# Own buffers for two tiles and one order edge in the seven-product pairs of a decoder layer

## The chip, the cores and the metric

The kernel runs on one core of a Trainium2 chip. A core has five engines that run beside one another, each with its own list of instructions that it takes in order: TensorE (PE, matrix products), VectorE (DVE), ScalarE (ACT), GpSimd (POOL) and SyncE (SP, which here issues loads and nothing else). Transfers between the memory of the chip and the core's own memory (SBUF) are done by 16 DMA engines; SyncE's and GpSimd's queues feed them. TensorE writes into PSUM, eight banks of 512 float32 in each of 128 partitions. The metric is the device time of one execution in microseconds (us); lower is better.

## The reference

One decoder layer on 512 tokens of width 1024 in float32: an input projection, block-sparse causal attention with a learned bias beside a causal mean-pool mixer, a gated merge and an output projection, a layer norm, and then the part that matters here, a gated MLP with 2816 inner channels and a causal convolution of width 3 on the gate:

```python
a, u = jnp.split(h @ w_ffn_in[l], 2, axis=-1)      # each (512, 2816)
a = causal_dwconv(a, conv_w[l], conv_b[l])
f = (jax.nn.gelu(a, approximate=False) * u) @ w_ffn_out[l]
h = layer_norm(ALPHA * h + f, ln2_g[l], ln2_b[l])
```

## The kernel before

Every product is made in three passes to keep float32 accuracy on faster matmuls: an operand is split into a high half (a rounded copy, by ScalarE) and a low half (what the copy lost, by VectorE), and TensorE adds high x high, high x low and low x high. So each weight tile of 128 x 1024 goes through the same path: a load into a raw buffer (tag `wraw`, three slots), a copy into `whi` by ScalarE (line 69), a difference into `wlo` by VectorE (line 70), and then matmuls. `whi` and `wlo` are rings of five slots each. The helper `split` issues the two, `mm3` (lines 182 to 186) the three matmuls.

The 2816 channels of `a` and of `u` are 22 tiles of 128. Tile f of `a` and tile f of `u` make a pair. Pairs 0 to 3 and 18 to 21 are computed plainly. For the pairs 4 to 17 (`SEVEN`) the two products are seen as one product of 2 x 2 blocks, the weights of `a` and `u` cut by the upper and lower half of the 1024 inputs and the tokens by halves of 256, and it is made with seven block products in place of eight, as Winograd and Strassen do. `seven(f)` (line 693) issues them, each of 12 matmuls of 256 columns. A pair needs four weight tiles:

- A: the weights of `a`, loaded (line 146).
- X: a sum of both weights, made by the DMA in two legs: a load of the weights of `u` by SyncE (line 131), and an accumulating load of the weights of `a` by GpSimd (line 132). It has a pool of its own, tag `xraw`, two slots. `fetch_sums` issues it some tiles ahead.
- D: the "quarter", half a tile of the weights of `u`, loaded (line 146), 128 x 512.
- Y: A plus parts of X, made by two sums of VectorE (line 144). The first needs X and A, the second A.

A, D and Y share the three slots of `wraw`. In the text the tile A of pair 12 is called A12, and so on. In the order of the loop a pair uses A, X, Y, A again, D, X again; the second use of Y, the closing product, is kept in the list `pending` and issued in the next pair. A and X have two products, Y two, D one.

The products land in three banks per pair (`sa`, `sb`, `sc`). The first product is copied by ScalarE into half of `y`, one of two tiles that alternate between pairs and that later hold the gate's convolution and activation (`gated`, lines 623 to 628). VectorE adds the parts (lines 708 to 711, "small adds"), the convolution takes two steps (lines 624 and 625) and the product with `u` one (line 628). VectorE also makes some sums of finished tiles for the product behind (lines 757 and 763).

The order of each engine's list isn't the order of the code. The kernel is built by a scheduler that knows what each instruction needs and which slot it takes, estimates times by a model of its own, and places the instructions of all engines by them. A slot is given to the next tile in the scheduler's order, and the wait for its last user is set with a semaphore. `keep_in_program_order` adds an edge: the instruction stays behind the one that was issued before it in the code on the same engine.

Of the kernel before, what the change touches and what calls it, by code (L numbers as in the profile page):

```python
# [8 lines left out]
F32 = mybir.dt.float32  # L9
F32R = mybir.dt.float32r  # L10
AF = mybir.ActivationFunctionType
ALU = mybir.AluOpType
PSUM = bass.MemoryType.PSUM

P = 128
S = 512
D = 1024
# [28 lines left out]
def layer_kernel(ctx: ExitStack, tc: tile.TileContext, xT, x, w_v, w_c, rel_bias, invcnt, w_group,  # L46
                 pscale, w_br, w_out, lnr, w_fi, convp, w_fo, out):
    nc = tc.nc
    const = ctx.enter_context(tc.tile_pool(name="const", bufs=1))
    wp = ctx.enter_context(tc.tile_pool(name="wp", bufs=1))  # L50
# [7 lines left out]
    def bank(name):  # L58
        return ps.tile([P, S], F32, tag="ps", name=name)
# [5 lines left out]
    def split(hi, lo, src, copy=None):  # L65
        if copy:
            copy(hi, src)
        else:
            nc.scalar.activation(hi, src, AF.Copy)  # L69
        nc.vector.tensor_tensor(lo, src, hi.bitcast(F32), op=ALU.subtract)  # L70
# [27 lines left out]
    def fetch(pool=None, early=None):  # L98
        i = state["next"]
        state["next"] = i + 1  # L100
        while sums and xu and fi_at[sums[0], "X"] <= i + AHEAD:
            fetch_sums(sums.pop(0))
        if isinstance(chunks[i], tuple):
            ready[i] = (fetch_fo if i >= FO0 else fetch_seven)(i, *chunks[i])
            return
        raw = wp.tile([P, D], F32, tag="wraw", name=f"wraw{i}", bufs=3)
        if pool is None:
            hi = wp.tile([P, D], F32R, tag="whi", name=f"whi{i}", bufs=RING)
            lo = wp.tile([P, D], F32R, tag="wlo", name=f"wlo{i}", bufs=RING)
        else:  # L110
            hi = pool.tile([P, D], F32R, name=f"whi{i}")
            lo = pool.tile([P, D], F32R, name=f"wlo{i}")
        parts = 2 if early else 1
        for c in range(parts):
            sl = slice(c * (D // parts), (c + 1) * (D // parts))
            (nc.scalar if early else nc.sync).dma_start(raw[:, sl], chunks[i][:, sl])
            split(hi[:, sl], lo[:, sl], raw[:, sl], fast if early and c == 0 else None)
            if c == 0 and early:
                early()
        ready[i] = (hi, lo)  # L120

    raws = {}
    sums = list(SEVEN)
    xu = None

# [9 lines left out]
    def fetch_seven(i, f, q):  # L135
        n = S if q == "D" else D
        if q == "X":
            raw = raws[f, "X"]
        else:
            raw = raws[f, q] = wp.tile([P, D], F32, tag="wraw", name=f"wraw{i}", bufs=3)[:, :n]  # L140
        if q == "Y":
            a, x_ = raws[f, "A"], raws[f, "X"]
            for c, o in ((slice(0, S), x_[:, S:]), (slice(S, D), raw[:, :S])):
                nc.vector.tensor_tensor(raw[:, c], o, a[:, c], op=ALU.add)
        elif q != "X":
            nc.sync.dma_start(raw, w_fi[2 * f] if q == "A" else w_fi[2 * f + 1][:, S:])
        hi = wp.tile([P, D], F32R, tag="whi", name=f"whi{i}", bufs=RING)[:, :n]
        lo = wp.tile([P, D], F32R, tag="wlo", name=f"wlo{i}", bufs=RING)[:, :n]
        split(hi, lo, raw)
        return hi, lo  # L150
# [26 lines left out]
    def weights(i):  # L177
        while state["next"] <= min(i + LEAD, state["limit"]):
            fetch()
        return ready[i]  # L180

    def mm3(out_, w, a, start, stop, **kw):
        (wh, wl), (ah, al) = w, a
        nc.tensor.matmul(out_, wh, ah, start=start, stop=False, **kw)  # L184
        nc.tensor.matmul(out_, wh, al, start=False, stop=False, **kw)  # L185
        nc.tensor.matmul(out_, wl, ah, start=False, stop=stop, **kw)  # L186

    def split3(v, a):
        return tuple(t.rearrange("p (a c) -> p a c", a=a) for t in v)
# [83 lines left out]
    for kt in range(KT):  # L273
        wh, wl = split3(weights(kt // 2), 2)
        wh, wl = wh[:, kt % 2, :], wl[:, kt % 2, :]
        xs_ = [(xT_hi[:, kt, j * P:(j + 1) * P], xT_lo[:, kt, j * P:(j + 1) * P]) for j in range(NT)]
        last = kt == KT - 1
        if last:
            for j in range(NT):
                mm3(bs[j], xs_[j], (wh, wl), False, True)  # L280
                nc.scalar.activation(vv[:, j, :], bs[j], AF.Copy)
        else:
            for n, (a, b) in enumerate(((0, 0), (1, 0), (0, 1))):
                for j in range(NT):
                    nc.tensor.matmul(bs[j], xs_[j][a], (wh, wl)[b], start=kt == 0 and n == 0, stop=False)  # L285
# [50 lines left out]
    def pool_out(j):  # L336
        b = bank(f"zb{j}")
        mm3(b, (wg_hi[:, j, :], wg_lo[:, j, :]), dif[j], True, True)
        nc.scalar.activation(zT[:, j, :], b, AF.Copy, scale=psc[:, j:j + 1])

    def in_tile(n):
        kind, j = order[n]
        wh, wl = split3(weights(C0 + n), KT)
        b = bank(f"{kind}{j}")
        for kt in range(KT):
            mm3(b, (wh[:, kt, :], wl[:, kt, :]), (xT_hi[:, kt, :], xT_lo[:, kt, :]), kt == 0, kt == KT - 1)
        if kind == "q":
            q_done(j, b)
        elif kind == "k":
            k_done(j, b)  # L350
        elif kind == "p":
            pool_in(j, b)
        elif len(gslot) < NKEEP:
            gslot[j] = gates[:, len(gslot), :]
            nc.vector.tensor_copy(gslot[j], b)
        else:
            gslot[j] = late[:, len(gslot) - NKEEP, :]
            nc.scalar.activation(gslot[j], b, AF.Sigmoid)
# [106 lines left out]
    for f in range(KT):  # L465
        if f == KT - LEAD:
            state["limit"] = WO0 + RING - 1
        wh, wl = split3(weights(BR0 + f), KT)
# [31 lines left out]
    ytiles = [ypool.tile([P, S], F32, name=f"y{j}") for j in range(2)]  # L500
# [120 lines left out]
    def gated(j, a, u, sign=None):  # L621
        y = ytiles[j % 2]
        nc.scalar.activation(y, a, AF.Identity, bias=cvp[:, j, 3:4], scale=cvp[:, j, 2:3])
        nc.vector.scalar_tensor_tensor(y[:, 1:], a[:, :S - 1], cvp[:, j, 1:2], y[:, 1:], op0=ALU.mult, op1=ALU.add)  # L624
        nc.vector.scalar_tensor_tensor(y[:, 2:], a[:, :S - 2], cvp[:, j, 0:1], y[:, 2:], op0=ALU.mult, op1=ALU.add)
        nc.scalar.activation(y, y, AF.Gelu)
        if sign:
            nc.vector.scalar_tensor_tensor(fT[:, j, :], y, sign, u, op0=ALU.mult, op1=ALU.mult)
        else:
            nc.vector.tensor_tensor(fT[:, j, :], y, u, op=ALU.mult)  # L630
# [20 lines left out]
    t1, t2 = slice(0, 256), slice(256, 512)  # L651
# [27 lines left out]
    for n in ("nT1", "T3", "nT2", "T4"):  # L679
        t_form(n)  # L680
    state["limit"] = len(chunks) - 1
    pending = []

    def s_mm(f, q, part, act_, b, start, skip=True):
        wh, wl = split3(weights(fi_at[f, q]), 4 if q == "D" else KT)
        for k in range(4):
            mm3(b, (wh[:, 4 * part + k, :], wl[:, 4 * part + k, :]), (act_[0][:, k, :], act_[1][:, k, :]),
                start and k == 0, k == 3, skip_group_check=not start)

    def whole(k, t):  # L690
        return hT_hi[:, k, t], hT_lo[:, k, t]

    def seven(f):
        ba, bb, bc = (bank(f"s{q}{f}") for q in "abc")
        chain, low, c11 = ba[:, 256:], bb[:, :256], bc[:, :256]
        y = ytiles[f % 2]
        u = xu.tile([P, S], F32, tag="u", name=f"u{f}", bufs=2)
        s_mm(f, "A", 0, whole(k1, t1), chain, True)
        nc.scalar.activation(y[:, t1], chain, AF.Copy)
        s_mm(f, "X", 0, tt["T3"], low, True)  # L700
        nc.scalar.activation(u[:, t2], low, AF.Copy)
        if pending:
            pending.pop()()
        s_mm(f, "Y", 0, tt["nT2"], chain, False)
        nc.scalar.activation(u[:, t1], chain, AF.Copy)
        s_mm(f, "A", 1, whole(k2, t1), c11, True)
        s_mm(f, "D", 0, tt["T4"], low, False)
        nc.vector.tensor_tensor(u[:, t1], u[:, t1], low, op=ALU.add)
        s_mm(f, "X", 1, tt["nT1"], chain, False)
        nc.vector.tensor_tensor(u[:, t2], u[:, t2], chain, op=ALU.add)  # L710
        nc.vector.tensor_tensor(ba[:, t1], y[:, t1], c11, op=ALU.add)

        def close():
            s_mm(f, "Y", 1, whole(k2, t2), chain, False)
            gated(f, ba, u, -1.0)

        pending.append(close)
# [3 lines left out]
    xu = xus.enter_context(tc.tile_pool(name="xu", bufs=1, reuse_waits="tile"))  # L721
# [211 lines left out]
```

## Time and profile before

| | |
|---|---|
| median of 3 runs | 650.57 us (650.09 to 651.02) |
| profiled execution | 649.74 us, of which the span from the first to the last instruction is 648.0 |
| TensorE busy | 635.7 us, 98% of the span |
| VectorE, ScalarE, GpSimd busy | 449.5, 328.0, 111.6 us |
| loaded and stored | 94.79 MB |

The profile was taken in one execution by the hardware. A row of the page or of a timeline has the engine, the line of the kernel, the operation and the tiles written and read, with buffer numbers left out (`whi` for each of its tiles); in a timeline the first two numbers are the start and the duration, in us from the start of the span, and brackets hold the idle time of the engine before it and what ended it. The chain of waits follows the work that ended last back to what released each step. A table of windows gives for a stretch the busy time of PE, PE's weight loads, DVE, ACT and POOL, each with its number of instructions in brackets, then the granted clock, the share of the DMA and GB/s. Matmuls are pipelined, so the time from one start to the next says more than their duration.

### The profile page before, as it was taken

The numbers are of one execution on the slowest core, as the hardware profiler recorded it, in microseconds if no ns is written. First come the engines' busy times: TensorE is split into PE (matmuls) and PEld (weight loads), VectorE is DVE, ScalarE is ACT, GpSimd is POOL, SyncE is SP. The second block draws the span as 40 slices with busy tenths as digits, with TensorE's granted clock in tenths as the row PEclk, the third lists the DMA queues.
The fourth block names the chain that finished last, engine by engine and source line by source line (L and its number), as shares of the span: only waits on it lengthen the run. The fifth ranks groups of instructions, "written<-read, shape, count | busy, mean of one in ns | idle before, by whom it ended". The sixth has DMA issues, their size and how long they took to land.

```text
span 648.0 us, 9322 instructions
## 1 busy us (share of the span) xinstructions
PE 635.7 (98%) x3586; PEld 551.4 (85%) x3586; DVE 449.5 (69%) x666; ACT 328.0 (51%) x475; POOL 111.6 (17%) x153
## 2 busy tenths in 40 slices
PE   9999999999999999999999999999999999999994
PEld 6888787877888888888999999998998888888884
DVE  6466665564532576299667888787986859698596
ACT  6547556675522333215444556455665337465452
POOL 1605361211000123300010101010100201123302
PEclk9999999999999999999999999999999999999998
DMA  9643222212222227404056686677635895989905
GB/s 323 197 166 99 82 81 82 74 67 89 74 95 98 91 98 286 136 1 162 2 150 173 170 208 155 179 179 188 165 128 163 274 264 137 218 188 193 282 4 129
DMA packets 32540, 94.79 MB, mean 146 GB/s; under 512 B 3688, under 2 KB 3944, under 8 KB 32240
## 3 DMA queue, kind: packets, MB, share of 16 engines
q1 hardware_dynamic: 22832, 66.91, 30.4%
q0 software_dynamic: 9088, 26.24, 20.7%
q10 hardware_dynamic: 576, 1.05, 0.5%
q8 instruction: 28, 0.46, 0.3%
q14 instruction: 16, 0.13, 0.1%
HBM read 91.02 MB, written 3.17 MB: 145 GB/s over the span
## 4 chain that ended last, share of the span: by engine, by line
PE 91%; DVE 3%; POOL 2%; DMA 1%; ACT 1%; issue 1%; DVEq 0%; ACTq 0%; POOLq 0%
PE fi L186 5%; PE fi L184 5%; PE fi L185 5%; PE g L184 5%; PE g L186 4%; PE g L185 4%; PE sa L184 4%; PE sa L186 4%; PE sa L185 4%; PE v L285 3%; PE wo L186 2%; PE br L186 2%; PE br L184 2%; PE wo L184 2%; PE wo L185 2%; PE br L185 2%
## 5 line engine op out<-in xcount | busy, mean ns | idle before, releaser
L70 DVE TENSOR_TENSOR wlo<-wraw,whi 128x1024 fp32r<-128x1024 f32 (+1 forms) x119 | 144.1, 1214 | 59.2 <-ACT whi L69 57.7
L69 ACT ACTIVATE whi<-wraw 128x1024 fp32r<-128x1024 f32 (+1 forms) x118 | 117.2, 996 | 131.9 <-PE g L185 23.6
L186 PE MATMUL fi<-hT_hi,wlo 128*128 128x512 f32 (+1 forms) x168 | 56.7, 339 | 0.0
L185 PE MATMUL fi<-hT_lo,whi 128*128 128x512 f32 (+1 forms) x168 | 56.7, 339 | 0.0
L184 PE MATMUL fi<-hT_hi,whi 128*128 128x512 f32 (+1 forms) x168 | 56.4, 340 | 0.0
L184 PE MATMUL g<-xT_hi,whi 128*128 128x512 f32 x128 | 50.3, 393 | 0.0
L186 PE MATMUL g<-xT_hi,wlo 128*128 128x512 f32 x128 | 49.9, 390 | 0.0
L185 PE MATMUL g<-xT_lo,whi 128*128 128x512 f32 x128 | 49.8, 389 | 0.0
L132 POOL DMA_DIRECT2D xraw<-in_w_fi x14 | 17.0, 1215 | 183.7 <-DVE y L624 70.2
L69 ACT ACTIVATE whi<-tw 128x1024 fp32r<-128x1024 f32 (+1 forms) x30 | 29.4, 982 | 21.6 <-DMA tw<-in_w_fo 8.1
L70 DVE TENSOR_TENSOR wlo<-tw,whi 128x1024 fp32r<-128x1024 f32 (+1 forms) x30 | 33.3, 1127 | 8.4 <-ACT whi L69 8.4
L185 PEld LDWEIGHTS fi<-hT_lo,whi 128*128 128x128 f32 x168 | 31.9, 190 | 3.5
L186 PEld LDWEIGHTS fi<-hT_hi,wlo 128*128 128x128 f32 x168 | 31.9, 190 | 3.3
L184 PEld LDWEIGHTS fi<-hT_hi,whi 128*128 128x128 f32 x168 | 31.6, 190 | 3.3
L184 PE MATMUL sa<-hT_hi,whi 128*128 128x256 f32 x112 | 31.9, 285 | 2.0 <-ACT whi L69 1.9
L186 PE MATMUL sa<-hT_hi,wlo 128*128 128x256 f32 x112 | 31.7, 284 | 0.0
L185 PE MATMUL sa<-hT_lo,whi 128*128 128x256 f32 x112 | 31.6, 283 | 0.0
L184 PE MATMUL sb<-T_hi,whi 128*128 128x256 f32 x112 | 31.5, 282 | 0.0
L184 PE MATMUL sa<-nT_hi,whi 128*128 128x256 f32 x112 | 31.5, 281 | 0.0
L186 PE MATMUL sa<-nT_hi,wlo 128*128 128x256 f32 x112 | 31.3, 279 | 0.0
L185 PE MATMUL sa<-nT_lo,whi 128*128 128x256 f32 x112 | 31.3, 279 | 0.0
L185 PE MATMUL sb<-T_lo,whi 128*128 128x256 f32 x112 | 31.3, 279 | 0.0
(250 smaller groups left out, 1762.8 us busy)
## 6 DMA issues: line engine op xcount, KB each, us to landing
wraw<-in_w_fi SPq DMA_DIRECT2D x30, 512.0 KB, 3.6
wraw<-in_w_c SPq DMA_DIRECT2D x28, 512.0 KB, 3.4
tw<-in_w_fo POOLq DMA_DIRECT2D x20, 512.0 KB, 8.3
xraw<-in_w_fi SPq DMA_DIRECT2D x14, 512.0 KB, 4.9
xraw<-in_w_fi POOLq DMA_DIRECT2D x14, 512.0 KB, 5.7
wraw<-in_w_fo SPq DMA_DIRECT2D x10, 512.0 KB, 5.1
tw<-in_w_fo SPq DMA_DIRECT2D x10, 512.0 KB, 6.6
wraw<-in_w_br SPq DMA_DIRECT2D x8, 512.0 KB, 3.3
```

The costliest lines, as they stand in the source:

```text
L69: nc.scalar.activation(hi, src, AF.Copy)
L70: nc.vector.tensor_tensor(lo, src, hi.bitcast(F32), op=ALU.subtract)
L132: nc.gpsimd.dma_start(v, bass.AP(tensor=a.tensor, offset=a.offset, ap=[[pst, pn], [u.offset + S - a.offset, 2], [est, S]]), accum_op=ALU.add)
L184: nc.tensor.matmul(out_, wh, ah, start=start, stop=False, **kw)
L185: nc.tensor.matmul(out_, wh, al, start=False, stop=False, **kw)
L186: nc.tensor.matmul(out_, wl, ah, start=False, stop=stop, **kw)
L285: nc.tensor.matmul(bs[j], xs_[j][a], (wh, wl)[b], start=kt == 0 and n == 0, stop=False)
```

## The change

The D tile gets a buffer of its own (`draw`, one slot, in the pool of X), so that `wraw`'s three slots serve A and Y alone. The copy of the first product goes to a tile of its own (`p1`, two slots) instead of half of `y`. The first matmul of D's product gets an order edge on TensorE: it stays behind the matmul before it in the code, the last of the first tile's second product. The list `pending` is made earlier in the code, with no effect. The new buffers take 4 KB of each partition.

```diff
@@ fetch_seven
         if q == "X":
             raw = raws[f, "X"]
-        else:
-            raw = raws[f, q] = wp.tile([P, D], F32, tag="wraw", name=f"wraw{i}", bufs=3)[:, :n]
+        elif q == "D":
+            raw = xu.tile([P, S], F32, tag="draw", name=f"draw{f}", bufs=1)
+        else:
+            raw = raws[f, q] = wp.tile([P, D], F32, tag="wraw", name=f"wraw{i}", bufs=3)
@@ mm3
-    def mm3(out_, w, a, start, stop, **kw):
+    def mm3(out_, w, a, start, stop, pin=False, **kw):
         (wh, wl), (ah, al) = w, a
-        nc.tensor.matmul(out_, wh, ah, start=start, stop=False, **kw)
+        ins = nc.tensor.matmul(out_, wh, ah, start=start, stop=False, **kw)
+        if pin:
+            tc.keep_in_program_order(ins)
@@ s_mm
-                start and k == 0, k == 3, skip_group_check=not start)
+                start and k == 0, k == 3, q == "D" and k == 0, skip_group_check=not start)
@@ seven
-        y = ytiles[f % 2]
+        y = xu.tile([P, 256], F32, tag="p1", name=f"p1f{f}", bufs=2)
...
-        nc.scalar.activation(y[:, t1], chain, AF.Copy)
+        nc.scalar.activation(y, chain, AF.Copy)
...
-        nc.vector.tensor_tensor(ba[:, t1], y[:, t1], c11, op=ALU.add)
+        nc.vector.tensor_tensor(ba[:, t1], y, c11, op=ALU.add)
```

The change adds three lines ahead of these places, so line 69 and 70 stay, the sums of Y become line 147, the loads of X lines 132 and 133, and the matmuls of `mm3` lines 187, 190 and 191.

More of the change, by code (lines that the diff above doesn't have):

```diff
@@ L122, in layer_kernel @@
     raws = {}
+    pending = []
     sums = list(SEVEN)
@@ L681, in layer_kernel @@
     state["limit"] = len(chunks) - 1
-    pending = []
     def s_mm(f, q, part, act_, b, start, skip=True):
```

## The prediction

> **What bounds the kernel now.** I read the page first, then the list of waits of TensorE, then the busy time of the stage of the pairs (from 348.0 us of the span), then the chain of waits, and last the timelines of VectorE, SyncE and GpSimd around the few places where TensorE stood.
>
> ```profile
> span 648.0 us, 9322 instructions
> PE 635.7 (98%) x3586; PEld 551.4 (85%) x3586; DVE 449.5 (69%) x666; ACT 328.0 (51%) x475; POOL 111.6 (17%) x153
> ...
> PE sa L184 <- ACT whi L69: 1.9, 2, 1.1
> ...
> 350.00:400.00 50.00, 50.00 (x423) 50.00 (x422) 41.40 (x57) 29.28 (x44) 4.83 (x4) 1.00 0.72 183
> 400.00:450.00 50.00, 47.96 (x396) 47.14 (x395) 41.17 (x58) 28.24 (x43) 6.02 (x5) 1.00 0.67 171
> 450.00:500.00 50.00, 50.00 (x387) 48.37 (x386) 40.62 (x56) 29.16 (x43) 2.41 (x2) 1.00 0.56 162
> ```
>
> TensorE is the bound: 635.7 of 648.0 us. In the stage of the pairs it issues 423 matmuls in 50.00 us where nothing holds it, 118.2 ns for one of 256 columns, so a product of 12 takes 1.42 us and a pair of 84 takes 9.93 us. VectorE is the next: 41.40 of 50 us. In the whole stage TensorE stands in one window alone, 47.96 of 50, and the list of waits names two waits for a split by ScalarE, 1.9 us together. These are the two:
>
> ```profile
> 404.28 1.74 DVE wlo L70 x2
> 406.03 4.74 DMA wraw<-in_w_fi
> 410.86 1.07 ACT whi L69
> 411.97 0.39 PE sa L184
> ...
> 410.84 0.28 PE L186 MATMUL sb<-T_hi,wlo 128*128 128x256 f32 x1
> ...
> 442.23 1.06 ACT L69 ACTIVATE whi<-wraw 128x1024 fp32r<-128x1024 f32 x1 [0.40 <-PE sc L185]
> ...
> 441.98 0.28 PE L186 MATMUL sc<-hT_hi,wlo 128*128 128x256 f32 x1
> 443.34 0.39 PE L184 MATMUL sa<-hT_hi,whi 128*128 128x256 f32 x1 [1.08 <-ACT whi L69]
> 443.56 0.28 PE L185 MATMUL sa<-hT_lo,whi 128*128 128x256 f32 x1
> 443.95 0.39 PE L184 MATMUL sa<-hT_hi,whi 128*128 128x256 f32 x1
> ```
>
> The first four lines are the chain: VectorE's work ends at 406.02 with the split of D10, whose slot A11 takes; only then the load of A11 is issued, it lands after 4.74 us, its high half is made in 1.07 us, and TensorE, whose last matmul had begun at 410.84, starts A11 at 411.97. The others: A13's last matmul begins at 441.98, the split of A14 takes over A13's slot in the ring of high halves, starts at 442.23, and TensorE starts A14 at 443.34, 1.36 us after its last start; from 443.56 to 443.95 it steps 0.39. Against the pace of 0.118 these are 1.0, 1.24 and 0.27: 2.5 us that a change of buffers and order can win here. Nothing else stands in the stage.
>
> **The change, part by part.** Instructions are neither added nor removed (3488 of TensorE, 139 of SyncE and 122 of GpSimd in both programs); buffers and order are what moves.
>
> *Own buffer for D.* A and Y now share three slots. A load of A waits for the low-half split of the Y two pairs earlier, no longer for work on the pair just before it (the split of D10, or in other pairs the second sum of a Y). For A11 that is the split of Y9, the row 401.31 below, which ended the first of its two splits at about 402.5: the load goes out some 3.5 us earlier, more than the 1.0 that TensorE stood. Gain 1.0. SyncE's queue keeps its three loads a pair; in three places A's now stands ahead of X's, in time with what it waits for. The D load of pair 4 moves behind the X loads of pairs 4 and 5, from 327.27 to about 329.5 (rows below), against a split of D4 at 342.75; hidden by those 13 us, without which pair 4's fifth product would wait. D's one slot makes its load wait for the split of the D before; behind it on the queue stands the next A, which waits longer for its own slot (D12 for about 420, A13 for about 423 in the walk below), so it holds nobody up.
>
> *Own buffer for the first product's copy.* ScalarE no longer waits for the activation of two pairs before. It is busy 29 us of 50, so this is worth nothing on the path; the cover is ScalarE's idle time.
>
> *The order edge.* D's product comes behind the first tile's second product and runs as 12 in a row. 84 matmuls a pair stay 84: cost nothing by itself, but D is no longer a filler that TensorE can take early.
>
> *The ring of high halves.* In the new program the shortest way from the last use of a slot to the first use of its next tile is 13 matmuls, 1.5 us, against 1.06 for the split, where A14 had 1 matmul. Gain 1.24 + 0.27. Together with A11: 2.5 us won.
>
> *VectorE's order, which the diff does not show.* With a slot free early, the two sums that make a Y are placed almost a pair earlier. In the old program Y12's first sum stands behind the split of A12, just ahead of X12's split. In the new one the sums of Y12, Y13, Y14 and Y15 stand ahead of the splits of X11, X12, X13 and X14 (and those of Y6 and Y7 ahead of X5 and X6). A sum needs its X whole in memory, and VectorE runs in order: behind a waiting sum stand the X split, the small adds that empty PSUM, and D's and Y's splits, and TensorE waits for their low halves. That X is loaded in two legs, the second an accumulation on GpSimd's queue, and the first is issued when the X two pairs earlier has been split, since X has two slots. These rows price it:
>
> ```profile
> 401.31 2.35 DVE L70 TENSOR_TENSOR wlo<-wraw,whi 128x1024 fp32r<-128x1024 f32 x2
> 404.19 1.22 DVE L70 TENSOR_TENSOR wlo<-xraw,whi 128x1024 fp32r<-128x1024 f32 x1
> 405.32 0.68 DVE L70 TENSOR_TENSOR wlo<-wraw,whi 128x512 fp32r<-128x512 f32 x1
> 405.43 0.38 SPq L131 DMA_DIRECT2D xraw<-in_w_fi  x1
> 410.09 1.20 POOL L132 DMA_DIRECT2D xraw<-in_w_fi  x1 [8.22 <-DMA xraw<-in_w_fi]
> 423.53 0.68 DVE L144 TENSOR_TENSOR wraw<-xraw,wraw 128x512 f32<-128x512 f32 x1
> 424.13 0.68 DVE L628 SCALAR_TENSOR_TENSOR fT<-y,u 128x512 f32<-128x512 f32 x1
> 424.73 1.22 DVE L70 TENSOR_TENSOR wlo<-xraw,whi 128x1024 fp32r<-128x1024 f32 x1
> ...
> 418.79 0.38 SPq L131 DMA_DIRECT2D xraw<-in_w_fi  x1
> 422.97 1.20 POOL L132 DMA_DIRECT2D xraw<-in_w_fi  x1 [11.68 <-DVE y L625]
> 425.98 0.38 SPq L131 DMA_DIRECT2D xraw<-in_w_fi  x1
> 431.94 1.20 POOL L132 DMA_DIRECT2D xraw<-in_w_fi  x1 [7.77 <-DVE wlo L70]
> ...
> xraw<-in_w_fi POOLq DMA_DIRECT2D x14, 512.0 KB, 5.7
> ```
>
> X10's split ends at 405.41, X12's load is issued at 405.43, its second leg at 410.09, and a second leg takes 5.7 us at the median: 10.4 us from split to whole. Before, the sum of Y12 came at 423.53, long after; the wait is not there to be seen, so it has bounds: 4.18 + 5.7 = 9.9 us (418.79 to 422.97) and 5.96 + 5.7 = 11.7 (425.98 to 431.94). I take 10.4: X12's load went out 0.6 us ahead of A11's (406.03) and not behind it, and in the new order A's load, which waits for an earlier split, is off the queue some us before X's. Were it under 8.0 us, no sum would wait, and the change would gain.
>
> [...]
>
> So a turn is: split of one X, 10.4 us, first sum of the Y two pairs on (0.60 to the next start), split of the X between: 1.22. That is 12.2 us a turn where TensorE wants a pair each 9.93, and in four turns in a row (from X10's split to X14's) and two at the start each turn loses 2.3 us less what slack there was. Durations for the rest of VectorE's work, and the two anchors:
>
> ```profile
> L70 DVE TENSOR_TENSOR wlo<-wraw,whi 128x1024 fp32r<-128x1024 f32 x34 | 41.5, 1222 | 7.6 <-ACT whi L69 7.0
> L624 DVE SCALAR_TENSOR_TENSOR y<-sa,cvp,y 128x511 f32<-128x511 f32 x14 | 10.4, 745 | 0.0
> L144 DVE TENSOR_TENSOR wraw<-wraw,wraw 128x512 f32<-128x512 f32 x13 | 8.9, 687 | 0.1
> L70 DVE TENSOR_TENSOR wlo<-wraw,whi 128x512 fp32r<-128x512 f32 x13 | 8.9, 687 | 4.4 <-ACT whi L69 4.2
> L708 DVE TENSOR_TENSOR u<-u,sb 128x256 f32<-128x256 f32 x14 | 5.8, 418 | 4.7 <-PE sb L186 4.1 <-issue 0.4
> ...
> 342.75 0.69 DVE L70 TENSOR_TENSOR wlo<-wraw,whi 128x512 fp32r<-128x512 f32 x1
> ...
> 327.27 0.33 SPq L146 DMA_DIRECT2D wraw<-in_w_fi  x1
> 328.54 14.69 SPq L131 DMA_DIRECT2D xraw<-in_w_fi  x3
> ...
> 347.75 1.20 POOL L132 DMA_DIRECT2D xraw<-in_w_fi  x1 [10.45 <-DMA xraw<-in_w_fi]
> ...
> L184 PE MATMUL sa<-hT_hi,whi x112: 277/283/387, 348.0 to 499.2; 128*128 128x256 f32 x112
> ```
>
> Neighbours on VectorE overlap by about 0.08 us: from 404.19 to 405.32 a split steps 1.13, from 423.53 to 424.13 a sum and from there to 424.73 a product 0.60. So I step a D split 0.60 too, a convolution step (lines 624 and 625) 0.66 and a small add 0.33, and let the last of a chain have its full 1.22.
>
> A low half is wanted at its tile's third matmul, counted in the new order at 118.2 ns each from 348.0, stalls so far added. Start: X6 is whole at 347.75 + 5.7 = 353.4; both sums of Y6 and X5's split end at 355.7; X7 is whole 10.4 later, 366.1; Y7's sum and X6's split end at 367.9, and TensorE wants that at 348.0 + 171 matmuls = 368.2: just in time. But Y6's split, six instructions on, ends at 372.6 where it is wanted at 372.2: 0.4. X8 is whole at 378.3, and Y7's split, nine instructions behind Y8's first sum, ends at 383.6 where it is wanted at 382.5: 1.1. For pairs 8 to 10 the sums stand behind the X split, with a wait of up to 1 us that the idle time of VectorE swallows.
>
> From X10's split, at 406.1 now: X12 is whole at 416.5; Y12's two sums and X11's split end at 418.9 (wanted 419.7, no loss); then two small adds, two convolution steps, D11's split and Y11's split end at 422.7, wanted at 421.8: 0.9. X13 whole at 429.3, X12's split ends 431.1: 0.6; Y12's split 434.8: 1.6. X14 whole at 441.5, X13's split 443.3: 0.1; Y13's split 447.3: 2.6. X15 whole at 453.7, X14's split 455.5: 0.6; A15's split 0.4. X16 whole at 465.9, its sum stands ahead of D15's and Y15's splits: 0.6 and 1.2. For pair 17 the sum stands behind the splits again. The sum of the stalls is 0.4 + 1.1 + 0.9 + 0.6 + 1.6 + 0.1 + 2.6 + 0.6 + 0.4 + 0.6 + 1.2 = 10.1 us.
>
> Net: 10.1 - 2.5 = 7.6 us more. The profiled execution took 649.74 us (648.0 of span and 1.74 around it), so 657.3 for it; it lies 0.83 under the median of the runs, 650.57, so 658.2 for the median. The same walk with 10.0 and 11.0 us for the X load gives 8.0 and 15.3 us of stalls. So the bound 9.9 gives about 7.5, less 2.5: 655.6; and 11.7 gives 15.3 + 0.7 for each of seven turns, less 2.5: 668.3.
>
> **The rivals.** *Faster: the loads are early enough.* The place is the first sum of Y12 on VectorE; it decides at 8.0 us, the time from the end of X10's split, 406.1 in the walk, to that of A11's, 414.1, behind which the sum stands. Under it no sum waits, the 2.5 us are won and the time is 648.1. For it: a VectorE that waits thins the traffic, and the loads of A have moved away. Against it: no X in the rows came under 9.9. Chance 0.10. [...]
>
> *No difference.* The waits are there but the stalls come to the 2.5 us that are won, 650.6. That takes an X load near 8.9 us, the walk's stalls falling by 5 for each us below 10; the shortest seen is 9.9. Chance 0.04.
>
> *Slower by much: loads collide.* A's load now goes out beside the accumulation of another X. If the second leg stretches, the time is that of the upper bound, 668. For it: the DMA share is 0.72 already in the window from 350; against it: 5.7 us is the median over all 14 legs in just that traffic. Chance 0.08. *The forecast*, 658.2, has the rest, 0.78.
>
> **How the numbers follow.** Of a change of 0.2% (1.3 us) a measurement of this kernel can tell little from none; the runs lie 650.09 to 651.02. Slower holds 0.78 + 0.08 = 0.86, same 0.04, faster 0.10. The range leaves out the two cases below (0.14) and the far end of the collision: its lower end is 652.5, 3 us under the bound 655.6 for splits that I put too late, its upper 665, where an X load takes about 11.2 us.
>
> **What would show it.** In the changed profile VectorE stands before the first sums (line 147) for the DMA of xraw, some 2 to 5 us for each of pairs 7, 8 and 12 to 16, about 25 us in all; TensorE waits for wlo (line 70) of VectorE, which it never did before, some 10 us between 370 and 475 us of the span; the waits for whi at A11 and A14 are gone. X's splits lie about 12 us apart in pairs 10 to 14. If VectorE does not stand at line 147, the reason is wrong; if it stands there but TensorE does not, my wanted times are; if a leg takes 4 us, the price is.

## The result and the profile after

| | median, us | runs | ratio to before, 95% interval |
|---|---|---|---|
| before (beside the changed kernel) | 650.77 | 650.09 to 651.02 | |
| changed kernel | 673.0 | 672.63 to 674.34 | 1.0347 [1.0329, 1.0365] |

The changed kernel is 22 us slower. The forecast, 658.2 us, had the sign and the mechanism but a third of the size, and its range (652.5 to 665) doesn't hold the time. The page of the profile first, its span, the line of TensorE and the first line of the chain of waits:

```profile
span 671.0 us, 9311 instructions
...
PE 642.6 (96%) x3586; PEld 555.3 (83%) x3586; DVE 446.9 (67%) x666; ACT 327.4 (49%) x475; POOL 110.8 (17%) x153
...
PE 73%; DMA 11%; DVE 9%; issue 3%; POOL 2%; ACT 2%; DVEq 0%; POOLq 0%; ACTq 0%
```

The span grew by 23.0 us, but TensorE's busy time by 6.9 only, and the other engines are as busy as before: the rest is time in which TensorE stands. The list of waits names it. A row has the instruction that waits, what released it, the sum in us, the count and the longest. Before, the first sums of Y had one wait for X, at pair 4, ahead of the stage of the pairs:

```profile
DVE wraw L144 <- DMA xraw<-in_w_fi: 4.9, 1, 4.9
```

In the changed kernel:

```profile
DVE wraw L147 <- DMA xraw<-in_w_fi: 32.0, 8, 5.0
...
DVE wraw L147 <- DMA wraw<-in_w_fi: 8.5, 4, 3.4
...
PE sa L191 <- DVE wlo L70: 6.6, 5, 2.3
...
PE sa L187 <- ACT whi L69: 3.9, 2, 3.4
...
PE sa L187 <- DVE sa L714: 3.7, 3, 2.3
...
PE sb L191 <- DVE wlo L70: 3.0, 4, 1.6
...
PE fod L190 <- DVE wlo L70: 1.0, 1, 1.0
```

VectorE stands 40.5 us at the first sums of Y (line 147): 32.0 us for X (4.3 of them at pair 4), and 8.5 us in the pairs 9 to 12 for the load of A, which lands there some 1.3 us after X. TensorE waits for low halves (line 70) in three of the rows, 10.6 us, of which 1.0 is in the output product (`fod`); the prediction said some 10. But it also waits 3.9 us for high halves and 3.7 us for the small add of line 714, which the prediction had not. The windows, in the columns that were explained for before:

```profile
350.00:400.00 50.00, 45.46 (x379) 44.86 (x378) 34.61 (x49) 25.39 (x39) 4.83 (x4) 1.00 0.62 146
400.00:450.00 50.00, 44.30 (x363) 43.20 (x363) 34.18 (x49) 25.56 (x40) 4.82 (x4) 1.00 0.62 161
450.00:500.00 50.00, 43.06 (x326) 41.83 (x326) 36.18 (x52) 23.46 (x36) 3.61 (x3) 0.93 0.49 130
```

In 50 us TensorE now issues 379 and 363 matmuls where it issued 423 and 396, and in the third window the granted clock is 0.93: here something comes in that no part of the prediction spoke of.

Two turns from VectorE's timeline show the mechanism as the prediction drew it:

```profile
368.74 0.69 DVE L147 TENSOR_TENSOR wraw<-xraw,wraw 128x512 f32<-128x512 f32 x1 [4.96 <-DMA xraw<-in_w_fi]
369.35 1.22 DVE L70 TENSOR_TENSOR wlo<-xraw,whi 128x1024 fp32r<-128x1024 f32 x1
...
382.38 0.69 DVE L147 TENSOR_TENSOR wraw<-xraw,wraw 128x512 f32<-128x512 f32 x1 [3.82 <-DMA xraw<-in_w_fi]
...
386.28 0.43 DVE L714 TENSOR_TENSOR sa<-p1f,sc 128x256 f32<-128x256 f32 x1
...
438.20 0.69 DVE L147 TENSOR_TENSOR wraw<-xraw,wraw 128x512 f32<-128x512 f32 x1 [4.97 <-DMA xraw<-in_w_fi]
438.80 1.22 DVE L70 TENSOR_TENSOR wlo<-xraw,whi 128x1024 fp32r<-128x1024 f32 x1
...
450.91 0.69 DVE L147 TENSOR_TENSOR wraw<-xraw,wraw 128x512 f32<-128x512 f32 x1 [4.51 <-DMA xraw<-in_w_fi]
451.52 1.22 DVE L70 TENSOR_TENSOR wlo<-xraw,whi 128x1024 fp32r<-128x1024 f32 x1
```

At 438.20 Y13's first sum has waited 4.97 us for X13; behind it X12 is split, until 440.02; only then X14's slot is free, and the sum of Y14 starts at 450.91. Turn: 12.7 us, where TensorE wants 9.93. The X load in it is 10.9 us, near the 10.4 assumed. But in the earlier pairs it is longer: X6's split ends at 370.57, X8's sum starts at 382.38, 11.8 us. Over the pairs 7 to 17 the median of this time, up to the landing of X, is 11.7 us (10.5 to 12.6). Measured in the same way it was 11.0 us before (9.9 to 12.2; 10.6 to 11.2 in the pairs 6 to 11), so the 10.4 was low for the kernel before too. The DMA issues of the page show what grew, the second leg: 5.7 us before and 6.7 us now, while the first leg fell from 4.9 to 4.0:

```profile
xraw<-in_w_fi SPq DMA_DIRECT2D x14, 512.0 KB, 4.0
xraw<-in_w_fi POOLq DMA_DIRECT2D x14, 512.0 KB, 6.7
```

TensorE's timeline around two of its stalls, one of each new kind:

```profile
384.20 0.28 PE L190 MATMUL sa<-nT_lo,whi 128*128 128x256 f32 x1
386.76 0.39 PE L187 MATMUL sa<-hT_hi,whi 128*128 128x256 f32 x1 [2.29 <-DVE sa L714]
...
454.19 0.28 PE L190 MATMUL sa<-nT_lo,whi 128*128 128x256 f32 x1
456.77 0.58 PE L191 MATMUL sa<-nT_hi,wlo 128*128 128x256 f32 x1 [2.30 <-DVE wlo L70]
457.15 0.42 PE L187 MATMUL sa<-nT_hi,whi 128*128 128x256 f32 x1
457.37 0.41 PE L190 MATMUL sa<-nT_lo,whi 128*128 128x256 f32 x1
```

The first is a closing product, Y6's second. It writes columns 256 to 511 of the bank `sa`, the small add of line 714 columns 0 to 255 of the same bank. The matmul waits 2.29 us for the add all the same, and the add (at 386.28, above) stands on VectorE behind Y8's sum, which waits 3.82 us for X8. Whether it is the shared bank that makes the matmul wait isn't shown: no run here puts the two into different banks. The second stall is of the kind that was foreseen (Y13's low half; 2.46 us against the pace of 0.118, 2.6 foreseen). After it the matmuls step 0.22 us and not 0.118. Windows cut at the two places where this happens:

```profile
456.80:460.20 3.40, 3.40 (x16) 3.40 (x17) 2.33 (x4) 0.89 (x3) 1.14 (x1) 0.50 0.50 186
...
484.10:487.50 3.40, 3.40 (x18) 3.40 (x18) 1.40 (x2) 0.81 (x1) 0.00 (x0) 0.50 0.93 293
```

Twice the granted clock is 0.50 for 3.4 us, each time just behind a stall (of 2.46 and 3.59 us), and costs about 1.5 us.

The longest stall, 3.71 us from start to start at 479.05, takes a third way, which ScalarE's timeline shows:

```profile
481.13 0.63 ACT L631 ACTIVATE y<-y 128x512 f32<-128x512 f32 x1 [5.21 <-DVE y L630]
481.67 1.99 ACT L69 ACTIVATE whi<-wraw 128x1024 fp32r<-128x1024 f32 x2
```

ScalarE's activation of the gate waits 5.21 us for VectorE's second convolution step, which stands behind the sum of Y16, and behind the activation stand the high halves of Y15 and A16. So a wait on VectorE reaches TensorE through ScalarE's list too.

Added up from the steps of TensorE's matmuls, the stage of the pairs loses 24.3 us against its pace: 19.4 in 14 stalls, 3.1 at half clock, 1.8 in the slower first steps behind a stall. Before it lost 3.6. The rest of the 23.0 us is a later start of the stage (0.6) and the output product (1.7, with the wait of `fod` above).

### The profile page after: what moved, and what is told of

The parts are those of the page before. It is cut to its first block, busy times and chain, and to the rows that moved or that the text cites. A ratio compares the mean times of both kernels' runs of the same rounds, so it can differ in the third digit from the quotient of the medians.

```text
span 671.0 us, 9311 instructions
## 1 busy us (share of the span) xinstructions
PE 642.6 (96%) x3586; PEld 555.3 (83%) x3586; DVE 446.9 (67%) x666; ACT 327.4 (49%) x475; POOL 110.8 (17%) x153
## 4 chain that ended last, share of the span: by engine, by line
PE 73%; DMA 11%; DVE 9%; issue 3%; POOL 2%; ACT 2%; DVEq 0%; POOLq 0%; ACTq 0%
DMA xraw<-in_w_fi 6%; PE fi L191 4%; PE fi L190 4%; PE fi L187 4%; PE g L187 4%; PE g L191 4%; PE g L190 4%; DVE wlo L70 3%; DMA wraw<-in_w_fi 3%; PE v L290 3%; PE wo L191 2%; PE br L191 2%; PE br L187 2%; PE wo L187 2%; PE wo L190 2%
## 5 line engine op out<-in xcount | busy, mean ns | idle before, releaser
L70 DVE TENSOR_TENSOR wlo<-wraw,whi 128x1024 fp32r<-128x1024 f32 (+1 forms) x105 | 134.8, 1288 | 54.5 <-ACT whi L69 53.9
L69 ACT ACTIVATE whi<-wraw 128x1024 fp32r<-128x1024 f32 (+1 forms) x104 | 107.9, 1043 | 124.0 <-PE g L190 23.7
L147 DVE TENSOR_TENSOR wraw<-xraw,wraw 128x512 f32<-128x512 f32 x14 | 9.7, 691 | 40.5 <-DMA xraw<-in_w_fi 32.0
L191 PE MATMUL sb<-T_hi,wlo 128*128 128x256 f32 x112 | 32.5, 290 | 3.0 <-DVE wlo L70 3.0
L631 ACT ACTIVATE y<-y 128x512 f32<-128x512 f32 x22 | 13.9, 630 | 40.8 <-DVE y L630 40.8
```

## The experiments

The theory: the first sums of Y are placed ahead of X splits, and VectorE, in order, waits there for a load of two legs. So it takes both, the early place and an X load over some 8 us; either alone costs nothing. The rivals: the buffers or the traffic cost by themselves, or the order edge does, or VectorE's new order does whatever X takes. In the first kernels one part of the change is made alone.

**D's own buffer alone** (on the kernel before):

```diff
-        else:
-            raw = raws[f, q] = wp.tile([P, D], F32, tag="wraw", name=f"wraw{i}", bufs=3)[:, :n]
+        elif q == "D":
+            raw = xu.tile([P, S], F32, tag="draw", name=f"draw{f}", bufs=1)
+        else:
+            raw = raws[f, q] = wp.tile([P, D], F32, tag="wraw", name=f"wraw{i}", bufs=3)
```

> The kernel before with D's own buffer alone, no tile of its own for the first product's copy, no order edge. Theory (VectorE stands in order at the first sum of a Y until both legs of its X have landed): the built program has the sums of Y6, Y7 and Y12 ahead of the split of the X before, those of Y13 to Y15 only just behind it. So the start loses as in the changed kernel (about 5 us to pair 8) and pairs 11 and 12 some 4, the rest little: 657 to 662 us, with about 20 us of VectorE's waits for xraw. Rival (the loss needs the copy's own tile or the edge, TensorE's order): 650 us. Rival (loads collide because A's go out early): as the changed kernel, about 673.

Measured: 662.05 us (661.0 to 663.15), ratio 1.0174 [1.0157, 1.019], at the upper end of the range that was expected; VectorE's waits for X, expected at about 20 us, are 15.3. Its list of waits:

```profile
DVE wraw L147 <- DMA xraw<-in_w_fi: 15.3, 4, 4.9
...
PE sa L187 <- DVE sa L714: 6.6, 5, 2.7
...
PE sb L191 <- DVE wlo L70: 1.6, 1, 1.6
```

Four sums that wait for X instead of eight, and half of the loss. With this buffer alone the sums of Y6, Y7 and Y12 stand ahead of an X split; Y13 to Y15 join when the copy has its own tile too. Of TensorE's waits here some three quarters are closing products behind the small add.

**The copy's own tile alone:**

```diff
-        y = ytiles[f % 2]
+        y = xu.tile([P, 256], F32, tag="p1", name=f"p1f{f}", bufs=2)
...
-        nc.scalar.activation(y[:, t1], chain, AF.Copy)
+        nc.scalar.activation(y, chain, AF.Copy)
...
-        nc.vector.tensor_tensor(ba[:, t1], y[:, t1], c11, op=ALU.add)
+        nc.vector.tensor_tensor(ba[:, t1], y, c11, op=ALU.add)
```

> The kernel before with the first product's copy in its own tile alone; D stays in the shared slots, no order edge. Theory: every sum stays nine VectorE instructions behind the split of the X before, as in the kernel before, so nothing waits for xraw; the shortest way round the ring of high halves is 13 matmuls (1 before), so the stall at A14 goes: 648 to 650.8 us. Rival (the copy's tile reorders TensorE to its harm): above 653.

Measured: 648.76 us (647.93 to 650.95, ten runs), ratio 0.9973 [0.9962, 0.9984]: faster than both kernels. Its sums stand where they stood before, 6 to 11 VectorE instructions behind the X split. Of the 2.5 us of old stalls, that of A14 is gone, that of A11 is still there with 0.6 us of wait. So this part, which the prediction gave as worth nothing on the path, is the only one that pays when made alone, though not for the reason weighed there (ScalarE's wait): the wait that went is one for a slot of the high halves, which the diff doesn't touch. Why the scheduler's order changed there wasn't tested.

**No order edge:** `q == "D" and k == 0` taken out of the changed kernel's call of `mm3`.

> The changed kernel without the order edge on TensorE. The lists of TensorE and VectorE are the same with and without it. So every theory that puts the loss on buffers and order expects the changed kernel again: 671 to 675 us, VectorE about 30 us before the first sums for xraw. The rival, that the edge takes away a filler and costs by itself, expects less: 650 to 668 us.

Measured: 670.88 us (670.22 to 671.55, two runs), ratio 1.0308 [1.0279, 1.0336], 0.1 us under the range that was expected. The edge doesn't make the loss. The interval overlaps with that of the changed kernel; whether the 2 us between the medians are anything isn't settled.

**The sums behind the splits.** The changed kernel with an edge on VectorE that holds a first sum behind the low-half split of the Y before:

```diff
-                nc.vector.tensor_tensor(raw[:, c], o, a[:, c], op=ALU.add)
+                add = nc.vector.tensor_tensor(raw[:, c], o, a[:, c], op=ALU.add)
+                if c.start == 0 and ysplit:
+                    tc.add_manual_dep(add.ins, ysplit[-1].ins.name, mybir.DependencyInfo(
+                        mybir.DependencyClass.NoSync, mybir.DependencyReason.DATA), reason="sum behind split")
...
-        split(hi, lo, raw)
+        low = split(hi, lo, raw)
+        if q == "Y":
+            ysplit.append(low)
```

> The changed kernel with one more order edge on VectorE: the first sum of a Y stays behind the low-half split of the Y of the pair before, where the shared slot used to hold it. All buffers and the edge on TensorE stay. Theory: VectorE's waits for xraw go (32 us to under 3), TensorE's waits for wlo and for the small add of line 714 go, both old stalls stay away: 648 to 650 us. Rival (the buffers or the loads that go out early are at fault): 660 to 673.

Measured: 652.35 us (650.1 to 654.04, twelve runs), ratio 1.0027 [1.0015, 1.0039]. All buffers are there, the order alone is put back, and 20.7 of the 22 us are gone. The waits that are left:

```profile
DVE wraw L148 <- DMA xraw<-in_w_fi: 2.2, 1, 2.2
...
PE sb L193 <- ACT whi L69: 1.3, 2, 0.7
...
PE fod L196 <- DVE wlo L70: 1.0, 1, 1.0
```

It missed the 648 to 650 that was expected: the two old stalls are gone, but others of the same size have come, for high halves and in the output product.

**The same with D's buffer alone:** the edge on the kernel before with D's own buffer, without the copy's tile.

> The kernel before with D's own buffer and the same edge on VectorE for all pairs. My theory: the buffer by itself costs nothing once the order is kept, and the load of A11 comes earlier: 648 to 652 us. Rival, that the buffer's place in SBUF or the earlier loads cost by themselves: 656 us or more.

Measured: 651.59 us (650.81 to 653.16), ratio 1.0017 [1.0008, 1.0027], against 662.05 without the edge. So neither the buffer's place nor the earlier loads cost by themselves. The gain of 2.5 us doesn't come either: the list of waits has 1.6 us for the copy into `y` (`ACT y L708`) and 1.0 us for a high half, in place of the old ones.

**Half of the pairs.** The edge with `and f < 12`, and with `and f >= 12` (there without the condition on `ysplit`).

> The changed kernel with the added edge on VectorE (first sum of a Y behind the low-half split of the Y before) only for pairs 5 to 11; from pair 12 on the sums are free, and stand ahead of the X splits in pairs 12, 14, 16 and 17. My theory, that each early sum costs where it stands: of the 24 us of stalls in the changed kernel those caused by Y7 to Y11 go (1.76 + 0.80 + 2.44 + 0.92 + 1.70, and 0.5 of restarts: 8 us), the others stay: 661 to 668 us. Rival, that the loss is one lag which is paid once, wherever the first early sums come: 671 us or more, or, if it is paid at the beginning only, under 654.

> The same edge for pairs 12 to 17 only. My theory: the 8 us caused by Y7 to Y11 stay, the 16 us behind them go (with the two stretches at half clock): 654 to 660 us, and no stretch at half clock. Rival as for the other half: 671 us or more, or under 654.

Measured: pairs 5 to 11 held, 660.41 us (659.2 to 662.28), ratio 1.0153 [1.0134, 1.0171]; pairs 12 to 17 held, 656.89 us (656.63 to 657.29), ratio 1.0095 [1.0078, 1.0112]. The second hit; its windows show the loss where the sums are free and none where they are held:

```profile
350.00:400.00 50.00, 45.58 (x357) 45.18 (x356) 33.66 (x47) 24.47 (x37) 4.83 (x4) 0.93 0.58 146
400.00:450.00 50.00, 48.94 (x413) 48.74 (x412) 41.12 (x59) 30.21 (x45) 4.82 (x4) 1.00 0.72 183
450.00:500.00 50.00, 50.00 (x408) 49.34 (x408) 41.56 (x60) 30.74 (x44) 3.62 (x3) 1.00 0.61 159
```

The first is 0.6 us below what was expected; why isn't shown. Its free half has another order than the changed kernel's (early at 12, 14, 16 and 17 instead of 12 to 15), but that was known when the range was given. Half clock came in both, once with the first half held and twice with the second, where I had expected none, each time within or just behind a stall (2.96 us between two matmul starts in the one, 2.15 and 2.82 in the other). The lag isn't paid once; each early sum costs at its own place.

**How long X takes.** Four kernels change the second leg. One leaves it out (X then lacks the weights of `a`), one cuts it to 64 of the 512 columns of each half (the rest of X lacks them), and one adds a third leg of 64 columns (which hold them twice), on the changed kernel and on the one with the copy's tile alone:

```diff
-        nc.gpsimd.dma_start(v, bass.AP(tensor=a.tensor, offset=a.offset,
-                                       ap=[[pst, pn], [u.offset + S - a.offset, 2], [est, S]]), accum_op=ALU.add)
+        nc.gpsimd.dma_start(v[:, :, :64], bass.AP(tensor=a.tensor, offset=a.offset,
+                                       ap=[[pst, pn], [u.offset + S - a.offset, 2], [est, 64]]), accum_op=ALU.add)
```

> The changed kernel without the accumulating second leg of X (so X lacks the weights of a; that part of the computation is left out). The built program has even more sums ahead of the X before (Y6, Y7, Y12 to Y17). Theory: X is whole 4 to 5.5 us after the split that frees its slot, a turn takes about 7 us, less than TensorE's 9.93, no sum holds TensorE up: 648 to 651 us. Rival (the order of VectorE or TensorE harms by itself, or a PSUM bank is freed late): 660 or more.

> The changed kernel with X's second leg cut to 64 of the 512 columns of each half (the other columns of X lack the weights of a). The first sums stay ahead of the X splits, for more pairs than before the cut. My theory, that the two legs of X together against VectorE's order make the loss, with the point of decision at 8.0 us of X load: the X load falls from 11.7 to 7 to 8.5 us, the time to 648 to 655 us, VectorE's wait for xraw at the first sums under 6 us. Rival, that the number of transfers and the hand-over between the two queues count and not their length: X load still over 10 us, 660 us or more.

> The changed kernel with a third leg behind the second, 64 of the 512 columns of each half once more (those columns of X hold the weights of a twice). My theory: some 2.5 us more of X load, to about 14 us, paid in 4 to 7 turns, so 10 to 18 us more than the changed kernel: 683 to 691 us. Rival, that the loss is the order of work on VectorE alone and its splits, and X is not what is waited for: the changed kernel again, 671 to 676 us.

> The kernel with the own tile for the first product's copy alone (first sums well behind the X splits, 648.76 us), with the same third leg. My theory: the same 2.5 us more of X load meet the slack of the old order, no more than 3 us lost: 648 to 652 us. Rival, that a longer X load or more traffic costs in any order (the DMA is the bound): 660 us or more.

Measured, with the X load as the median over the pairs 7 to 17 from the end of the X split two before to the landing of the last leg:

| kernel | sums ahead of X splits | X load, us | time, us | ratio, interval |
|---|---|---|---|---|
| one leg | pairs 6, 7, 12 to 17 | 3.5 | 649.66 (one run) | |
| small second leg | pairs 6, 7, 12 to 17 | 7.4 | 648.95 | 0.9975 [0.996, 0.999] |
| changed kernel | pairs 6, 7, 12 to 15 | 11.7 | 673.0 | 1.0347 [1.0329, 1.0365] |
| third leg | pairs 6, 12, 14, 16 | 14.5 | 691.96 | 1.0627 [1.0604, 1.065] |
| copy's tile alone | none | 10.2 | 648.76 | 0.9973 [0.9962, 0.9984] |
| the same, third leg | none | 16.4 | 649.39 | 0.9989 [0.9976, 1.0003] |

Three of the four times lie where they were expected; the third leg on the changed kernel came 1 us above its 683 to 691. With the small second leg VectorE's waits for X missed: 10.4 us, in six waits of at most 2.3 us, where under 6 us were expected. TensorE has one stall in that stage, of 0.6 us: short waits of VectorE were absorbed. The waits of the kernel with three legs and early sums:

```profile
DVE wraw L149 <- DMA xraw<-in_w_fi: 51.9, 11, 7.4
...
PE sa L193 <- DVE wlo L70: 16.8, 5, 5.3
...
PE sa L189 <- DVE sa L716: 8.6, 2, 4.8
...
PE sb L193 <- DVE wlo L70: 6.5, 2, 5.5
```

and of the kernel with three legs and the old order:

```profile
DVE wraw L147 <- DMA xraw<-in_w_fi: 14.1, 9, 4.9
...
PE sa L187 <- ACT whi L69: 0.8, 1, 0.8
```

The last is the clearest pair: X takes 16.4 us and VectorE stands 14.1 us at the first sums there too (4.9 of it at pair 4, ahead of the stage), but the X split isn't behind them, and TensorE waits 0.8 us in the whole stage. D's own buffer with the sums held points the same way: its X load is 12.7 us, longer than the changed kernel's, and its only wait for X is at pair 4. In the early order the loss begins between 7.4 and 11.7 us of X load; the line through the changed kernel and the third leg, 6.8 us of time for each us, meets the 649 of the kernels without loss at some 8.2 us. The prediction had 8.0. That they lie so close is in part luck, as sums stand ahead in six pairs of the one kernel and in four of the other.

## Why the prediction was wrong in size

*Held.* The early place of the sums, the wait for X and the turn are as predicted, and a threshold near 8.0 us fits the runs. The edge isn't the cause, as the run without it shows, and SyncE's queue with D's one slot holds no A up: A12's load goes out at 419.48 us, Y10's low half is done at 419.46. The 2.5 us of old stalls did go: A11 and A14 are no longer in the list. Stall by stall from pair 11 on, in us against the pace, predicted and measured: Y11 0.9 and 1.5; X12 0.6 and 1.0; Y12 1.6 and 1.4; X13 0.1 and 0.4; Y13 2.6 and 2.5; X14 0.6 and 0.5; A15 0.4 and 0.35; pair 15's D and Y 1.8 and 3.6, and 0.6 at A16: 8.6 against 11.8. Where the X load was near the assumed one, 10.5 to 10.8 us in the pairs 12 to 14, the walk over VectorE's list was right to 0.6 us. Its end wasn't.

*The step that failed* is the term of 10.4 us for the X load, and with it the walk's start, the sentences from "Start: X6 is whole" to "that the idle time of VectorE swallows". It gave the pairs 6 to 10 a loss of 1.5 us, and they lost 7.6: X6 1.76, the closing products of the pairs 5, 6 and 8 0.80, 2.44 and 0.92, and Y10 1.70. Three things were wrong in it. The X load there is 10.9 to 12.6 us and not 10.4. Some 0.6 us of that was there before the change: the 10.4 came from one row, X12's, and the median was 11.0. The rest is in the second leg, 6.7 us instead of 5.7. A longer second leg is what the rival "loads collide" named, and the load lies at that rival's bound; what stretches the leg wasn't tested, and it took 5.9 us with all the buffers and the sums held. Next, the walk took X as what a first sum waits for last. The sum of Y8 did wait for X, 3.8 us where the walk had up to 1. But the sums of Y9, Y10 and Y11 waited 1.3, 2.3 and 1.5 us, each of them at the end for A, some 1.3 us behind X; the stalls at the closing product of pair 8 and at Y10 come behind these. And it counted as wanted from VectorE only low halves. Its list "X split, the small adds that empty PSUM, and D's and Y's splits" has the small add in it, but the closing product was never asked when it needs that. The kernel with the pairs from 12 on held has just this start left, and lies 8.1 us over the copy's tile alone (656.89 less 648.76), 3.0 of them at half clock.

*Not in the prediction at all:* 3.1 us at half clock, 1.8 us of slow first steps behind stalls, and the way through ScalarE, 3.9 us of waits for high halves: Y15's 3.59 and A16's 0.61 against the pace. The prediction followed VectorE's list alone. The difference is made up so: 10.1 us were predicted; the start adds 6.1 (7.6 less 1.5), the rest of the walk 3.2 (11.8 less 8.6), half clock and restarts 4.9, together 24.3. Another 1.7 us are in the output product. With an X load of 11.7 us the prediction's own upper bound, 668.3, has 20.2 us of stalls (15.3 and 0.7 in each of seven turns), and 19.4 were measured. That this sum comes out is in part luck: some 8 us of the measured stalls are at closing products and at high halves, which the walk hadn't. What that bound lacks is the half clock and the restarts.

*The chances.* Slower had 0.86 and came. "Loads are early enough" fell at its own place: VectorE does stand at line 147, 32.0 us for X in all, and the legs took 4.0 and 6.7. But the first leg alone, with no second, took 3.5, and at 7.4 us of X load the kernel gave 648.95 where the prediction had 648.1 under the threshold.

## What to carry to other kernels

When a change frees a buffer, compare the order of every engine's list before and after: an instruction that comes to stand early, and needs a transfer, holds up all that is queued behind it on that engine (here VectorE at the first sums of Y, 32.0 us for X). Ask of each thing behind it who waits for it, and count all of them: the operand splits (TensorE waited 10.6 us for low halves), the adds that the next product waits for (3.7 us), and what an engine behind it holds up in turn (3.9 us for ScalarE's high halves). Make each part of a change alone: here D's buffer by itself made half of the loss, the copy's tile by itself was 0.27% faster than the kernel before but with D's buffer brought the other half, and the edge made at most some 2 us.

## What the runs showed of the chip

Short stalls of TensorE cost more than their length: in the changed kernel 4.9 us on top of the 19.4 of its 14 stalls, 3.1 at half clock and 1.8 in the first steps behind. In all of these kernels the granted clock, as the trace records it, fell to 0.5 in the stage of the pairs only within or just behind stalls, for 3.413 us or for twice that. In the kernels with one stretch or two it followed steps between matmul starts of 2.15 us (pairs from 12 on held), 2.58, 2.82, 2.96, 3.02, 3.45 and 3.71 us, but not one of 2.21 (without the edge) or 2.56 us (the changed kernel, at 384.20). So it isn't the length alone.

The traces go some way further. Within one kernel the starts of the stretches lie whole multiples of 3.413 us apart (8 in the changed kernel, 7 without the edge, 5 with the later pairs held). When the time is cut into pieces of 3.413 us that begin and end at these starts, the piece that ends where the clock falls has TensorE standing for 0.55 to 1.00 of it (by the idle times in brackets) in 13 of the 14 cases, and no piece at full clock without a fall behind it has more than 0.49, the two stalls of 2.21 and 2.56 us being cut in two by the grid. The one exception is the kernel with the pairs 5 to 11 held, where the clock fell a piece late, behind 0.55 and then 0.41. So a share of somewhat over half fits these 14 cases, but isn't settled, and what makes the clock fall isn't shown.

The accumulating leg's time depends on the kernel around it: for the same 512 KB its median was 5.5 us with the copy's tile alone, 5.7 before, 5.9 with all the buffers and the sums held, 6.7 in the changed kernel and 7.4 with D's buffer alone and the sums held. Which transfers beside it stretch it isn't shown.
